# Mixture-of-experts layer on one Trainium2 core: weight ring laid into the mixer's tiles, 17 steps of 128, 96+32 and 64+64 slots

## The chip, the cores and the metric

The kernel runs on 1 core of one Trainium2 chip. The metric is the device time of one execution in microseconds (us). Below, "step" is one pass through the expert loop, "tile of weights" is 1 MB (half of one expert's gate, up or down matrix), and "slot" is one row of an expert's batch of tokens.

## What is computed

Two layers over 512 latent tokens and 256 context tokens of width 1024 (layer 1's second part works on the 512 latent ones). Each layer has a mixer (attention, gating and neighbourhood branches, output projection, gated residual) and then a mixture of experts. The change touches the second part:

```
expert = two best of 8 experts in the best of 4 groups   # per token, 32 experts
hdn    = silu(xb @ w_gate[e]) * (xb @ w_up[e])           # 1024 -> 512
y      = hdn @ w_down[e]                                 # 512 -> 1024
out    = h + gate * sum over the token's two experts of (weight * y)
```

Everything is fp32. One expert has 3 matrices of 2 MB, so 6 tiles of 1 MB; 32 experts are 192 tiles, 201 MB, per layer, and every expert is read in every layer.

## The kernel before

**Router.** The mixer's last stage is an output projection in two column halves (lines 1405 to 1438); after each token tile of the second half the router's logits are added up in PSUM (line 1401). `Router.choose` (line 1521) then runs a chain of small VectorE operations with a few TensorE products between: the two experts of each token, each token's position within its expert (`pos_ps`, `pk`), the experts' counts and their ranks by count. The two experts with the numbers 0 and 1 are fixed (`NST = 2`): they get ranks 0 and 1 whatever their counts, so that their weights can be asked for before the routing is known. All others are ranked by count, and `eid` (line 1574) is the list of expert numbers by rank, from which the SyncE queue reads an expert's number with a register load (line 1722) before it issues that expert's weights. `fill` (lines 1513 to 1519) turns positions and ranks into the list of tokens of every step by a series of small TensorE products, and `index` (line 1607) writes it as integers `gi` (rows to gather) and `si` (rows to scatter to).

**Steps.** In layer 0 the first 8 ranks are solo steps of 128 slots (`SOLO`) and the other 24 make 12 pairs of 64 slots each: 20 steps. In layer 1 it is 6 solo steps and 13 pairs: 19 steps. The order starts with the two fixed experts, then mixes pairs and solos, and ends with a solo. Each step gathers its 128 rows (line 1787, GpSimd's indirect DMA), transposes them (line 1798, eight TensorE transposes), multiplies by gate and up (`gateup`, four half products through `product`, line 1808), and in the next step's time transposes the hidden rows (line 1827), multiplies by down (`down`, two halves) and scatters the rows (line 1844). In a pair the two experts' matmuls take 64 columns of TensorE each, the second at column 64 (`tile_position`), alternately for each slice k of the contraction. So the program on TensorE runs: products of step i, transposes for step i+1, down of step i-1.

**Weights.** `Stream` (line 1706) holds the tiles in order of use. A ring of 15 tiles (`RP, RE = 7, 8`) lies in pools of its own, which replace the mixer's. `ahead` (line 1742) is called behind every half product and asks for as many tiles as were used, all on SyncE's queue at line 1731. The tiles of the ring that the mixer's space gives up come free one by one during the output projection.

**Overflow.** Tokens beyond an expert's slots are worked off behind the last step in a loop (`For_i`), whose number of passes `further` (line 1617) computes.

Of the kernel before, what the change touches and what calls it, by code (L numbers as in the profile page):

```python
# [23 lines left out]
KC = 8  # L24
# [7 lines left out]
SOLO = (8, 6)  # L32
NST = 2
NOV = (23, 15)
# [78 lines left out]
def backbone(ctx: ExitStack, tc: tile.TileContext, a, out, dbg=None):  # L113
# [119 lines left out]
    def mixer(l, comb):  # L233
# [52 lines left out]
        def wsplit(i, most=2, way=0):  # L286

            while most and i not in gone:
                if i not in pre:
                    pump()  # L290
                pool = pool2["p"] if seq[i] in (("out", 2), ("out", 3)) else wp
                first = i not in ready
                if first:
                    ready[i] = (pool.tile([128, KC, 256], F32R, tag="wh", name="wh", bufs=2),
                                pool.tile([128, KC, 256], F32R, tag="wl", name="wl", bufs=2))
# [175 lines left out]
        vv = wp.tile([128, 4, 512], F32, name="vv", bufs=1) if last else vtile([128, 6, 512], "vv")  # L471
# [867 lines left out]
        wo = ts.enter_context(tc.tile_pool(name=f"wo{l}", bufs=1, side="left", reuse_waits="tile"))  # L1339
        pool2["p"] = wo  # L1340
# [65 lines left out]
        for n in range(2):  # L1406
# [34 lines left out]
        st.close()  # L1441
        route.stack = rqs
        return hs, route
# [17 lines left out]
    class Router:  # L1461


        def __init__(self, l, NT, rq):
# [3 lines left out]
            self.pos_ps, self.ips, self.rank_ps, self.erow_ps, self.cc = (  # L1468
                pi[:, :NT + 1], pi[:, NT + 1], pi[:, NT + 2], pi[:1, NT + 3], pi[:NE, NT + 4, 0:1])
# [7 lines left out]
            self.H = SOLO[l]  # L1477
            self.P = (NE - self.H) // 2
            self.ns = self.H + self.P
            self.gi = const.tile([C, SOLO[0] + (NE - SOLO[1]) // 2], I32, name="gi")[:, :self.ns]  # L1480
            self.si = const.tile([C, SOLO[0] + (NE - SOLO[1]) // 2], I32, name="si")[:, :self.ns]

# [30 lines left out]
        def fill(self, po, oh, out, n, pair=None):  # L1513

            up = [(out[:, :n], k, nt, slice(0, 128), slice(0, n)) for k in range(2) for nt in range(self.NT)]
            low = [(out[64:128, pair[0]], k, nt, slice(0, 64), pair[1]) for _, k, nt, _, _ in up] if pair else []
            parts = up[:1] + low + up[1:]
            for i, (o, k, nt, sl, cl) in enumerate(parts):
                PE.matmul(o, po[:, k, nt, sl], oh[:, k, nt, cl], start=(i == 0), stop=(i == len(parts) - 1))

        def choose(self):
# [39 lines left out]
            for nt in range(NT):  # L1561
                PE.matmul(self.cc, OHs[:, nt, :], onesb[:, 0:1], start=(nt == 0), stop=(nt == NT - 1))

# [11 lines left out]
            tmp = t_([2, NT, NE], "tmp")  # L1575
            V.tensor_mul(tmp, self.OH, self.pos_ps[:, None, :NT, :].to_broadcast([128, 2, NT, NE]))
            V.reduce_sum(self.pk, tmp, axis=AX.X)
            po = t_([2, NT, C], "po", F16)
            V.tensor_tensor(po, self.along(C), self.over(self.pk, C), op=ALU.is_equal)
# [4 lines left out]
            V.tensor_scalar(v, r, float(self.H), -64.0, op0=ALU.is_lt, op1=ALU.mult)  # L1584
            V.tensor_add(self.d, self.pk, v)
            V.tensor_scalar(v, self.d, 64.0, 99.0, op0=ALU.is_ge, op1=ALU.mult)
            V.tensor_add(r, r, v)
            oh = self.column(rp, r, NE, "oh")
            self.fill(po, oh, self.ips, self.ns, (slice(self.H, self.ns), slice(self.ns, NE)))
            self.index(rp, self.ips, self.ns, self.gi, self.si)  # L1590
# [16 lines left out]
        def index(self, rp, ps, n, gi, si):  # L1607

            ps = ps[:, :n]
# [7 lines left out]
        def further(self, rp):  # L1617
# [4 lines left out]
            most = -(-(NT * 128 - 64) // C)  # L1622
# [5 lines left out]
            V.tensor_scalar(past, self.rank, float(self.H), -64.0, op0=ALU.is_lt, op1=ALU.mult)  # L1628
            V.scalar_tensor_tensor(past, cnt, -64.0, past, op0=ALU.add, op1=ALU.add)
# [31 lines left out]
            V.tensor_scalar_add(d, d, -64.0)  # L1661
# [18 lines left out]
            self.index(rp, ips, nov, self.gv, self.sv)  # L1680


    def moe(l, hs, route):
# [4 lines left out]
        RP, RE = 7, 8  # L1688
        NRAW = RP + RE
        ms, es_ = ExitStack(), ExitStack()  # L1690
        p = ms.enter_context(tc.tile_pool(name=f"m{l}", bufs=1, side=SIDE[l][0], reuse_waits="tile"))
        ep = es_.enter_context(tc.tile_pool(name=f"e{l}", bufs=1, side=SIDE[l][1], reuse_waits="tile"))
        pp = es_.enter_context(tc.tile_pool(name=f"eps{l}", bufs=1, space=PSUM, reuse_waits="tile"))
        wview = [a[n][l].rearrange("e (p k) f -> e p k f", p=128) for n in ("w_gate", "w_up", "w_down")]
        KK = (8, 8, 4)
        H, P, ns = route.H, route.P, route.ns

        def raw_tile(tag):
            return p.tile([128, 2048], F32, tag=tag, name=tag, bufs=RP - 4 if tag == "ew" else 2)

        def ring(i):
            if i < RP:
                return raw_tile("ew" if i < RP - 4 else "en" if i < RP - 2 else "ex")
            return ep.tile([128, 2048], F32, tag="er", name="er", bufs=RE)

        class Stream:


            def __init__(self, units, regs=None):
                self.units, self.regs = units, regs  # L1710
                self.room = NRAW if regs is None else RE
                self.raw = {}
                self.nl = self.nu = 0

            def expert(self, x):

                if self.regs is not None:
                    return ds(self.regs[x], 1)
                if x < NST:
                    return slice(x, x + 1)  # L1720
                if x not in places:
                    places[x] = SP.value_load(route.eid[0:1, x:x + 1], min_val=0, max_val=NE - 1)
                return ds(places[x], 1)

            def loads(self, upto):
                while self.nl < min(upto, len(self.units)):
                    x, mat, half = self.units[self.nl]
                    kk = KK[mat] // 2
                    t = ring(self.nl % NRAW if self.regs is None else RP)
                    src = wview[mat][self.expert(x), :, half * kk:(half + 1) * kk, :]  # L1730
                    SP.dma_start(t.rearrange("p (k f) -> p k f", k=kk), src.rearrange("o p k f -> (o p) k f"))
                    self.raw[self.nl] = t.rearrange("p (k f) -> p k f", k=kk)
# [367 lines left out]
```

## Time and profile before

| what | value |
|---|---|
| median of 3 runs | 2704.84 us (2703.21 to 2708.1) |
| the profiled execution | 2701.97 us |
| its span on the core | 2700.2 us |
| TensorE busy | 2410.3 us (89%) |
| VectorE, ScalarE, GpSimd busy | 1145.2, 691.0, 442.7 us |
| mean granted TensorE clock | 0.963 |
| moved by DMA | 625.81 MB, mean 232 GB/s |
| read from HBM | 602.55 MB |

The span is the time from the first to the last event on the core; the execution's time has 1.8 us around it. TensorE (PE) has matmuls in the table of groups, and its weight loads run beside them. The share of busy time is a mean over the mixers and the expert layers, whose limits differ. The numbers by stretch stand below.

### The profile page before, as it was taken

To read this page: it belongs to the slowest core of one execution; us is meant where nothing else is said; L and a number is where in the kernel's file an instruction comes from. 1 tells how busy PE (TensorE), PEld (TensorE's weight loads), DVE (VectorE), ACT (ScalarE), POOL (GpSimd) and SP (SyncE) were. 2 spreads that over 40 slices of the span, in tenths; PEclk is the share of its full clock that TensorE was granted. 3 is DMA by queue.
4 is the path that set the end of the run, shared out by engine and by line. 5 is a ranking of instruction groups with operands and counts; after the bars stand their busy time and mean duration, and the time that the engine had idled before them with its cause. 6 is when DMAs were issued, how large, how long until landed. Compare 5 with 4: busy or idle time off the path is not lost. (4 is left out here: it accounts for less than half of the span.)

```text
span 2700.2 us, 33207 instructions
## 1 busy us (share of the span) xinstructions
PE 2410.3 (89%) x12789; PEld 1641.1 (61%) x12789; DVE 1145.2 (42%) x2076; ACT 691.0 (26%) x1350; POOL 442.7 (16%) x387
## 2 busy tenths in 40 slices
PE   5999899899999699999986899999999699998983
PEld 4888788788887443333334788887877543333331
DVE  3455768677745411111104647676554411110003
ACT  4234655522222100000002325555223100000001
POOL 0221210212211100100000313112332100000002
PEclk9999999999999799999997899999999799999997
DMA  5411211365424799999996411123554699999993
GB/s 240 125 56 37 70 59 44 126 222 173 150 100 182 255 352 420 420 421 418 411 410 247 156 63 52 36 89 129 214 193 166 257 342 419 419 416 412 411 415 147
DMA packets 118144, 625.81 MB, mean 232 GB/s; under 512 B 18880, under 2 KB 24768, under 8 KB 58976
## 3 DMA queue, kind: packets, MB, share of 16 engines
q1 hardware_dynamic: 93232, 576.61, 54.7%
q0 software_dynamic: 14528, 32.60, 3.5%
q10 hardware_dynamic: 10224, 14.46, 1.5%
q8 instruction: 102, 1.67, 0.3%
q14 instruction: 58, 0.48, 0.1%
HBM read 602.55 MB, written 40.96 MB: 238 GB/s over the span
## 5 line engine op out<-in xcount | busy, mean ns | idle before, releaser
L217 PE MATMUL pg<-xh,wh 128*128 128x512 f32 (+1 forms) x576 | 205.2, 356 | 0.0
L218 PE MATMUL pg<-xl,wh 128*128 128x512 f32 (+1 forms) x576 | 205.0, 356 | 0.0
L219 PE MATMUL pg<-xh,wl 128*128 128x512 f32 (+1 forms) x576 | 204.1, 354 | 0.0
L694 PE MATMUL pj<-xh,wh 128*128 128x512 f32 (+1 forms) x544 | 196.2, 361 | 7.5 <-DVE rt L814 2.8
L696 PE MATMUL pj<-xh,wl 128*128 128x512 f32 (+1 forms) x544 | 189.9, 349 | 1.4 <-DVE wl L638 1.4
L1844 POOL DMA_INDIRECT yb<-mx,si x39 | 41.9, 1075 | 901.1 <-DVE mx L1843 652.7
L695 PE MATMUL pj<-xl,wh 128*128 128x512 f32 (+1 forms) x544 | 189.1, 348 | 0.0
L1808 PE MATMUL pu<-er,mt 128*64 128x512 f32 (+1 forms) x560 | 159.5, 595 | 19.5 <-DMA er<-in_w_up 19.3
L1808 PE MATMUL pd<-er,mt 128*64 128x512 f32 (+1 forms) x568 | 171.3, 596 | 6.1 <-DMA er<-in_w_down 3.2
L350 DVE SCALAR_TENSOR_TENSOR jk<-wr,crow 128x1024 bf16<-128x1024 f32 x128 | 155.8, 1218 | 47.0 <-DMA wr<-in_w_adaT 44.7
L1821 DVE TENSOR_TENSOR mx<-mx,pu 128x512 f32<-128x512 f32 x39 | 26.8, 688 | 343.0 <-PE pu L1808 336.4
L1808 PE MATMUL pg<-er,mt 128*64 128x512 f32 (+1 forms) x488 | 157.9, 610 | 9.6 <-DMA er<-in_w_gate 9.6
L200 POOL TENSOR_TENSOR wl<-wr,wh 128x1024 fp32r<-128x1024 f32 x48 | 119.6, 2492 | 280.6 <-ACT wh L199 280.6
L1843 DVE COPY mx<-pd 128x512 f32<-128x512 f32 x39 | 27.0, 692 | 306.8 <-ACT mx L1842 298.9
L1820 ACT ACTIVATE mx<-pg 128x512 f32<-128x512 f32 x39 | 23.3, 597 | 479.5 <-PE pg L1808 479.5
L1307 ACT ACTIVATE sg<-pg 128x512 f32<-128x512 f32 x72 | 37.9, 527 | 369.0 <-PE pg L219 361.4
L923 PE MATMUL S<-K,Q 128*128 128x256 f32 (+3 forms) x544 | 117.9, 342 | 14.5 <-ACT E L961 6.1
L1830 DVE COPY mt<-trh 128x512 f32<-128x512 f32 x39 | 27.0, 691 | 240.8 <-PE trh L1827 240.8
L1808 PEld LDWEIGHTS pu<-er,mt 128*64 128x64 f32 (+1 forms) x560 | 50.5, 142 | 112.7 <-issue 74.7
L217 PEld LDWEIGHTS pg<-xh,wh 128*128 128x128 f32 x576 | 108.1, 188 | 17.4 <-issue 0.3
L218 PEld LDWEIGHTS pg<-xl,wh 128*128 128x128 f32 x576 | 108.7, 189 | 15.9
L219 PEld LDWEIGHTS pg<-xh,wl 128*128 128x128 f32 x576 | 108.1, 188 | 16.7
(373 smaller groups left out, 5347.4 us busy)
## 6 DMA issues: line engine op xcount, KB each, us to landing
er<-in_w_down SPq DMA_DIRECT2D x71, 1024.0 KB, 21.5
er<-in_w_up SPq DMA_DIRECT2D x70, 1024.0 KB, 20.4
er<-in_w_gate SPq DMA_DIRECT2D x61, 1024.0 KB, 20.9
wr<-in_w_in SPq DMA_DIRECT2D x54, 1024.0 KB, 4.8
wr<-in_w_adaT SPq DMA_DIRECT2D x80, 512.0 KB, 3.7
ew<-in_w_gate SPq DMA_DIRECT2D x28, 1024.0 KB, 21.1
ew<-in_w_up SPq DMA_DIRECT2D x26, 1024.0 KB, 21.9
ew<-in_w_down SPq DMA_DIRECT2D x24, 1024.0 KB, 21.6
```

The lines of the kernel that those rows point to most:

```text
L200: (eng or V).tensor_sub(lo, x, hi.bitcast(F32))
L217: PE.matmul(ps, lh, rh, start=(i == 0), stop=False)
L218: PE.matmul(ps, lh, rl, start=False, stop=False)
L219: PE.matmul(ps, ll, rh, start=False, stop=(i == n - 1))
L350: V.scalar_tensor_tensor(jk, ad["t"][:, i % 2 * D:(i % 2 + 1) * D], 1.0, ad["c"][:, s], op0=ALU.mult, op1=ALU.mult, accum_out=modT[al][:, ...
L694: PE.matmul(ps, lh, rh, start=(k == 0), stop=False)
L695: PE.matmul(ps, lh, rl, start=False, stop=False)
L696: PE.matmul(ps, ll, rh, start=False, stop=(k == KC - 1))
L923: PE.matmul(ps, q[:, m, part, c], K[:, m, ks], start=(part == 0), stop=(part == 1))
L1307: S.activation(sg[:, o:o + n], ps[:, :n], AF.Sigmoid)
L1808: PE.matmul(ps[r], lt[:, k0 + k, r], w[:, k, c], start=(k0 + k == 0), stop=(k0 + k == kk - 1), **pos)
L1844: G.indirect_dma_start(out=yb[l], out_offset=bass.IndirectOffsetOnAxis(ap=idx, axis=0), in_=y, in_offset=None, bounds_check=2 * TT - 1, oo ...
```

## The change

- **Steps.** 17 steps in both layers (`NS`). Ranks 0 and 3 (`ALONE`) are solo steps of 128 slots. Of the others the biggest, ranks 1, 2 and 4 onwards, six in layer 0 and eight in layer 1 (`WIDE`), get 96 slots and share their step with one of the six or eight smallest experts, which gets 32 slots. The rest are pairs of 64 slots: nine in layer 0 and seven in layer 1. Experts 0, 1, 2 are now fixed (`NST = 3`). The order is solo 0, the wide steps of ranks 1 and 2, then pairs with wide steps between and the second solo in the middle; the last step is a wide one.
- **Matmuls of a wide step.** For each k, `product` issues three: 64 columns at column 0 and 32 at column 64 for the big expert, 32 at column 96 for the small one.
- **The ring.** 16 tiles that lie in tiles of the mixer's own pools, plus 5 (layer 0) or 4 (layer 1) of a small pool. The first 16 units are all of fixed experts: gate and up of 0 and 1, down of 0, gate and up of 2, down of 1. `Stream` is made in the mixer's tail, which asks for 1 or 2 tiles behind its row loads, one more at token tiles 1 and 3 of the first half of the output projection and 4 at the last token tile of each half; the expert layer's start asks for the rest up to 16. From there a tile is asked for when the unit 16 places before it has been used.
- **The router's chain in three parts.** `choose` becomes a generator. Part one makes positions and the list of expert 0 alone, whose rows are gathered at once. Part two does ranks, `eid` and each token's column. Part three, behind step 0's first half product, runs `fill` for the other 16 steps (48 small products where there were 24 in layer 0, 32 for 16 in layer 1), then the lists and the gather of step 1.
- `room` gives 128, 96, 64 or 32 slots by rank, for the columns and for the overflow.

```diff
-SOLO = (8, 6)
-NST = 2
+WIDE = (6, 8)
+NST = 3
+ALONE = 3
+NS = NE // 2 + 1
...
+        ring = [(wx, "x", 1)] + ([(wp, "vv", 1)] if last else []) + [(wp, "wr1", 1), (wp, "wr0", 1)]
+        ring += [(wp, t, 2) for t in ("wh", "wl")] * 2 + [(wa, "o0", 1)] + [(wo, f"o{i}", 1) for i in (1, 2, 3)]
+        weights = Stream(l, route, plan_steps(l), ring)
+        weights.loads(2 if last else 1)
...
                 if n == 0 and nt in (1, 3):
                     wsplit(at["n"] + nt // 2)
+                    weights.loads(weights.nl + 1)
...
+                if nt == NT - 1:
+                    weights.loads(weights.nl + 4)
...
-        def fill(self, po, oh, out, n, pair=None):
+        def fill(self, po, oh, out, n, low=()):
-            up = [(out[:, :n], k, nt, slice(0, 128), slice(0, n)) for k in range(2) for nt in range(self.NT)]
-            low = [(out[64:128, pair[0]], k, nt, slice(0, 64), pair[1]) for _, k, nt, _, _ in up] if pair else []
+            kn = [(k, nt) for k in range(2) for nt in range(self.NT)]
+            up = [(out[:, :n], k, nt, slice(0, 128), slice(0, n)) for k, nt in kn]
+            lo = [(out[o:128, c], k, nt, slice(0, 128 - o), x) for o, c, x in low for k, nt in kn]
...
+        def room(self, v, r):
...
+            V.tensor_scalar(v, r, float(2 + self.W), None, op0=ALU.is_lt)
+            for x, op in ((NE - self.W, ALU.is_lt), (0, ALU.is_equal), (ALONE, ALU.is_equal)):
+                V.scalar_tensor_tensor(v, r, float(x), v, op0=op, op1=ALU.add)
...
+            oh = t_([2, NT, 1], "oh0", F16)
+            V.tensor_mul(oh, self.OH[:, :, :, 0:1], tokn[l].rearrange("p k (t o) -> p k t o", o=1))
+            self.fill(po, oh, self.ips0, 1)
+            self.index(rp, self.ips0, self.gi[:, 0:1], self.si[:, 0:1])
+            yield
...
+    def plan_steps(l):
...
+        W = WIDE[l]
+        solo = [((x, 0, 128),) for x in (0, ALONE)]
+        small = list(range(NE - W, NE))
+        wide = [((x, 0, 96), (small.pop(0), 96, 32)) for x in range(1, 2 + W) if x != ALONE]
+        pair = [((x, 0, 64), (x + NS - 2 - W, 64, 64)) for x in range(2 + W, NS)]
+        r = solo[:1] + wide[:2]
+        rest = [wide[2:], pair]
+        for i in range(len(pair)):
+            r.append(pair[i])
+            n = len(wide) - 2
+            r += wide[2 + i * n // len(pair):2 + (i + 1) * n // len(pair)]
+            if i == len(pair) // 2:
+                r.append(solo[1])
...
+        return r
...
+            fixed = [] if regs is not None else [u for u in use if u[0] < NST][:16]
+            self.units = fixed + [u for u in use if u not in fixed]
...
+        def ahead(self):
...
+            self.used.update(self.now)
+            self.now = []
+            n = len(self.ring)
+            while self.nl < len(self.units) and (self.nl < n or self.units[self.nl - n] in self.used):
+                self.loads(self.nl + 1)
...
-        st_ = Stream(order([members(j) for j in plan]))
-        st_.loads(6 * NST - 2)
-        route.choose()
-        st_.loads(NRAW)
+        st_.loads(16)
+        choice = route.choose()
+        next(choice)
...
             for k in range(n):
-                for i, w in enumerate(ws):
-                    r = slice(None) if len(ws) == 1 else HALVES[i]
-                    pos = {} if len(ws) == 1 else {"tile_position": (0, 64 * i)}
-                    PE.matmul(ps[r], lt[:, k0 + k, r], w[:, k, c], start=(k0 + k == 0), stop=(k0 + k == kk - 1), **pos)
+                for (_, o, r), w in zip(m, ws):
+                    for o, r in ((o, r),) if r != 96 else ((o, 64), (o + 64, 32)):
+                        pos = {} if r == 128 else {"tile_position": (0, o)}
+                        PE.matmul(ps[o:o + r], lt[:, k0 + k, o:o + r], w[:, k, c], start=(k0 + k == 0),
+                                  stop=(k0 + k == kk - 1), **pos)
...
         gather(xg[0], gi[:, 0:1])
+        next(choice)
         x = xpose(xg[0])
-        gather(xg[1], gi[:, plan[1]:plan[1] + 1])
...
-            def mid():
-                if i:
+            def mid(part):
+                if i == part == 0:
+                    assert next(choice, 0) == 0
+                    gather(xg[1], gi[:, plan[1]:plan[1] + 1])
+                if i and part == 1:
                     box["hh"] = hpose(hd)
```

On TensorE, at the first step of layer 0 with two experts, the rows before are these (`tr` are the transposes of gathered rows, `trh` of hidden rows, `pg` and `pu` the gate and up products, `pd` the down product; `ew`, `en`, `ex`, `er` are weight tiles):

```order
L1798 MATMUL tr<-ident,mx 128x128 x8
L1808 MATMUL pd<-er,mt 128x512 x8
L1808 MATMUL pg<-er,mt 64x512 x8
L1808 MATMUL pu<-er,mt 64x512 x8
L1827 MATMUL trh<-ident,mx 128x128 x4
L1808 MATMUL pg<-er,mt 64x512
L1808 MATMUL pg<-ew,mt 64x512
```

and with the change, whose first such step is the second of the layer:

```order
L1848 MATMUL pu<-ew,mt 128x512 x4
L1838 MATMUL tr<-ident,mx 128x128 x8
L1848 MATMUL pg<-ew,mt 64x512
L1848 MATMUL pg<-ew,mt 32x512 x2
L1848 MATMUL pg<-ew,mt 64x512
L1848 MATMUL pg<-ew,mt 32x512 x2
L1848 MATMUL pg<-ew,mt 64x512
L1848 MATMUL pg<-ew,mt 32x512 x2
```

A half product of a pair is eight matmuls of 64 columns; that of a wide step is four of 64 columns and eight of 32, in turns.

On SyncE's queue, where layer 0's first weights are asked for, the rows before are

```order
L1731 DMA er<-in_w_up 128x2048
L1731 DMA er<-in_w_down 128x2048 x2
L1722 TENSOR_LOAD eid
L1722 ISA x2
L1731 ISA
L1731 DMA er<-in_w_gate 128x2048
```

and with the change

```order
L1771 DMA ew<-in_w_up 128x2048
L1771 DMA ew<-in_w_down 128x2048 x2
L1771 DMA ew<-in_w_gate 128x2048
L1771 DMA ew<-in_w_up 128x2048
L1771 DMA ew<-in_w_gate 128x2048
L1771 DMA ew<-in_w_up 128x2048
L1771 DMA ew<-in_w_down 128x2048 x2
L1758 TENSOR_LOAD eid
L1758 ISA x2
L1771 ISA
L1771 DMA ew<-in_w_gate 128x2048
```

Ten tiles stand ahead of the first register load of `eid` before, sixteen with the change.

On VectorE, in layer 0's routing, from the ranks on (`route` is the router's scratch, `OH` the choice of each token), the rows before are

```order
L1571 TENSOR_SCALAR route<-io_79,route 32x32
L1574 CAST eid<-pps 1x32
L1576 TENSOR_TENSOR route<-OH,pps 128x384
L1577 TENSOR_REDUCE pk<-route 128x12
L1579 TENSOR_TENSOR route<-io_79,pk 128x1536
L1581 TENSOR_TENSOR route<-OH,pps 128x384
...
L1614 TENSOR_TENSOR gi<-route 128x20
```

and with the change

```order
L1588 TENSOR_TENSOR route<-OH,pps 128x384
L1589 TENSOR_REDUCE pk<-route 128x12
L1591 TENSOR_TENSOR route<-io_79,pk 128x1536
L1594 TENSOR_TENSOR route<-OH,tokn_81 128x12
L1644 TENSOR_SCALAR route<-pps 128x1
L1645 SCALAR_TENSOR_TENSOR route<-pps,route 128x1
L1646 TENSOR_SCALAR route<-pps 128x1
L1647 TENSOR_TENSOR gi<-route 128x1
L1648 CAST si<-route 128x1
L1600 SCALAR_TENSOR_TENSOR route<-pps,kcol 32x1
```

The positions (128x384, the reduction, 128x1536) moved ahead of the ranks (32x32 rows), and step 0's list `gi` comes before the ranks are begun.

## Rows read from the trace of the kernel before

**Rows 1.** Stretches: length; busy PE, PEld, DVE, ACT, POOL; PE clock, DMA share, GB/s.

```profile
840.00:902.00 62.00, 59.46 (x320) 50.27 (x318) 35.40 (x61) 10.08 (x24) 4.69 (x9) 1.00 0.45 156
902.00:935.00 33.00, 9.46 (x91) 8.30 (x91) 15.94 (x57) 2.19 (x4) 3.68 (x4) 0.52 0.83 321
935.00:980.00 45.00, 44.40 (x131) 20.11 (x132) 5.46 (x15) 4.82 (x7) 4.00 (x4) 0.97 0.80 262
980.00:1430.00 450.00, 419.69 (x1610) 165.75 (x1608) 56.74 (x109) 30.64 (x52) 34.17 (x32) 1.00 1.01 415
```

**Rows 2.** SyncE's queue, timeline (start us, us, operation): weight tiles asked for.

```profile
919.82 0.33 SPq L1731 DMA_DIRECT2D er<-in_w_gate  x1
973.95 3.91 SPq L1731 DMA_DIRECT2D er<-in_w_gate  x2
1405.66 10.30 SPq L1731 DMA_DIRECT2D er<-in_w_down  x5
2192.87 3.91 SPq L1731 DMA_DIRECT2D er<-in_w_gate  x2
2618.17 10.26 SPq L1731 DMA_DIRECT2D er<-in_w_down  x5
```

**Rows 3.** The page's list of DMA issues: KB each, median us to landing.

```profile
er<-in_w_down SPq DMA_DIRECT2D x71, 1024.0 KB, 21.5
```

**Rows 4.** TensorE, timeline: solo and pair steps of layer 1.

```profile
2154.39 4.44 PE L1808 MATMUL pg<-ew,mt 128*128 128x512 f32 x8
2158.67 3.60 PE L1808 MATMUL pu<-ew,mt 128*128 128x512 f32 x8
2162.10 3.60 PE L1808 MATMUL pg<-ew,mt 128*128 128x512 f32 x8
2170.63 3.67 PE L1808 MATMUL pg<-en,mt 128*128 128x512 f32 x8 [0.61 <-issue]
2192.77 3.65 PE L1808 MATMUL pg<-er,mt 128*64 128x512 f32 x16
2215.44 3.65 PE L1808 MATMUL pg<-ex,mt 128*64 128x512 f32 x16
```

**Rows 5.** Layer 0's routing and first step: VectorE, TensorE and GpSimd, timelines.

```profile
914.27 0.15 DVE L1565 SCALAR_TENSOR_TENSOR route<-pps,kcol 32x1 f32<-32x1 f32 x1 [1.23 <-PE pps L1562]
915.78 0.53 DVE L1576 TENSOR_TENSOR route<-OH,pps 128x384 f32<-128x384 bf16 x1
918.61 0.55 DVE L1581 TENSOR_TENSOR route<-OH,pps 128x384 f32<-128x384 bf16 x1
921.81 1.31 PE L1519 MATMUL pps<-route 128*128 128x20 f16 x24 [6.18 <-DVE route L1510]
924.83 1.10 POOL L1788 DMA_INDIRECT mx<-xs,gi  x1 [21.27 <-DVE route L1601]
933.23 1.97 PE L1798 MATMUL tr<-ident,mx 128*128 128x128 f32 x8 [10.11 <-DMA mx<-xs,gi]
935.14 4.78 PE L1808 MATMUL pg<-ew,mt 128*128 128x512 f32 x8
```

**Rows 6.** TensorE, timeline: the last down product of each layer.

```profile
1437.77 7.10 PE L1808 MATMUL pd<-er,mt 128*128 128x512 f32 x16 [1.45 <-issue]
2650.34 7.11 PE L1808 MATMUL pd<-er,mt 128*128 128x512 f32 x16 [1.45 <-issue]
```

**Rows 7.** TensorE, timeline: columns (128*64, 128*32) side by side, and a change of width.

```profile
25.60 2.12 PE L430 MATMUL adaps<-adw,cpad 128*32 128x128 f32 x64
1103.15 0.84 PE L1798 MATMUL tr<-ident,mx 128*128 128x128 f32 x6
1103.91 0.64 PE L1808 MATMUL pd<-ex,mt 128*64 128x512 f32 x1
1104.39 0.59 PE L1808 MATMUL pd<-ex,mt 128*64 128x512 f32 x1
```

**Rows 8.** The trace's DMA view, list of issues: the gathers.

```profile
mx<-xs,gi POOLq DMA_INDIRECT x39, 10.7
```

More of the change, by code (lines that the diff above doesn't have):

```diff
@@ L1338, in mixer, with second_tile @@
         ts = ExitStack()
-        wo = ts.enter_context(tc.tile_pool(name=f"wo{l}", bufs=1, side="left", reuse_waits="tile"))
-        pool2["p"] = wo
+        es_ = ExitStack()
+        wa = st.enter_context(tc.tile_pool(name=f"wa{l}", bufs=1, side="left", reuse_waits="tile"))
+        wo = es_.enter_context(tc.tile_pool(name=f"wo{l}", bufs=1, side="left", reuse_waits="tile"))
+        wx = es_.enter_context(tc.tile_pool(name=f"wx{l}", bufs=1, side="left", reuse_waits="tile"))
+        second = iter([(wa, "o0"), (wo, "o1"), (wo, "o2"), (wo, "o3")])
+        def second_tile(name):
+            p, tag = next(second)
+            return p.tile([128, KC, 256], F32R, tag=tag, name=name, bufs=1)
+        pool2["t"] = second_tile
         rp = ts.enter_context(tc.tile_pool(name=f"r{l}", bufs=1, side="left", reuse_waits="tile"))
@@ L1679, in further @@
             self.sv = const.tile([C, NOV[0]], I32, name="sv")[:, :nov]
-            self.index(rp, ips, nov, self.gv, self.sv)
-    def moe(l, hs, route):
+            self.index(rp, ips, self.gv, self.sv)
+    def plan_steps(l):
[12 more added lines that the diff above has]
+                r.append(solo[1])
+        assert sorted(x[0][0] for x in r) == list(range(NS)) and sorted(y[0] for x in r for y in x) == list(range(NE))
+        return r
@@ L1695, in moe @@
[L1695 to L1732, printed above, removed]
-                    self.nl += 1
-            def get(self, *want):
-                i = self.nu
-                assert self.units[i] == want, (self.units[i], want)
-                self.nu += 1
-                self.loads(i + 1)
-                return self.raw.pop(i)
-            def ahead(self):
-                self.loads(self.nu + self.room)
@@ L1745, in members @@
-        def members(j):
-            return (j,) if j < H else (j, j + P)
-        def order(steps):
-            def downs(m):
-                return [(x, 2, half) for half in range(2) for x in m]
-            r, prev = [], ()
-            for m in steps:
-                r += [(x, mat, half) for half in range(2) for mat in range(2) for x in m]
-                r += downs(prev)
-                prev = m
-            return r + downs(prev)
-        plan = list(range(NST))
-        solo, pair = list(range(NST, H)), list(range(H, ns))
@@ L1763, in moe @@
-        for i in range(len(pair)):
-            plan.append(pair[i])
-            if (i + 1) * len(solo) // len(pair) > i * len(solo) // len(pair):
-                plan.append(solo[(i + 1) * len(solo) // len(pair) - 1])
-        assert sorted(plan) == list(range(ns))
-        places = {}
+        ep = es_.enter_context(tc.tile_pool(name=f"e{l}", bufs=1, side="left", reuse_waits="tile"))
+        pp = es_.enter_context(tc.tile_pool(name=f"eps{l}", bufs=1, space=PSUM, reuse_waits="tile"))
+        st_.ring += [(ep, "er", (5, 4)[l])] * (5, 4)[l]
@@ L1770, in moe, with raw_tile @@
+        assert len(st_.ring) == 16
+        rows_ = {"en": [("wh", 2)], "ex": [("wl", 2)], "ew": [("vv" if last else "o0", 1), ("wr0", 1), ("wr1", 1)]}
+        held = {t: p for p, t, _ in st_.ring}
+        turn = {"n": 0}
+        def raw_tile(kind):
+            x = rows_[kind]
+            tag, bufs = x[turn["n"] % len(x)]
+            turn["n"] += kind == "ew"
+            return held[tag].tile([128, KC, 256], F32, tag=tag, name=kind, bufs=bufs).rearrange("p a b -> p (a b)")
         b0, b1 = [bt(i, [128, 3072], F32, "mx") for i in SH]
@@ L1814, in gateup @@
                 for mat, ps in ((0, pg), (1, pu)):
-                    product(ps, x, [st_.get(y, mat, half) for y in m], 4 * half, 4, KC)
+                    product(ps, x, m, [st_.get(y[0], mat, half) for y in m], 4 * half, 4, KC)
                     st_.ahead()
-                if half == 0 and mid is not None:
-                    mid()
+                    if mid is not None:
+                        mid(2 * half + mat)
             sl, hd = sl_[i % 2], hd_[i % 2]
@@ L1835, in down @@
             for half in range(2):
[L1836 removed]
+                ws = [st_.get(y[0], 2, half) for y in m]
                 for o in range(2):
                     c = slice(o * 512, o * 512 + 512)
[L1839 removed]
+                    product(pd[:, c], ht, m, ws, 2 * half, 2, 4, c)
                 st_.ahead()
```

141 lines of the change are left out of this document (88 added, 53 removed).

## The prediction, made before the changed kernel ran

> **What bounds the kernel now.** I read first the busy time by stretch [rows 1]. The change touches only the expert layers, so the question is what limits those. From 980 to 1430 us of layer 0 the DMA engines are full (share 1.01, 415 GB/s), while TensorE is busy 419.69 of 450 us: the weights set the pace. Only the first two steps, 935 to 980, are the other way round: TensorE is busy 44.40 of 45 us and the DMA moves 262 GB/s. Before them, from 902 to 935, the router's chain runs, and TensorE has 9.46 us of work in 33.
>
> The second view is SyncE's queue [rows 2], which tells when the DMA becomes the limit. The ring is full at 919.82, before the first product; from then on a tile is asked for when one was used. The 26th is asked for at 973.95 + 3.91 - 0.33 = 977.53, which is 42.4 us after the first product at 935.14 [rows 5]; in layer 1 at 2196.45, 42.1 us after 2154.39 [rows 2, 4]. From there the queue never runs dry: the last ask is at 1405.66 + 10.30 - 0.33 = 1415.63, and 21.5 us later [rows 3] it has landed, at 1437.1. The tiles 26 to 192, 167 of them, took 459.6 us, **2.752 us each**. Layer 1 gives 2628.10 + 21.5 = 2649.6, and 2.713 us each. The five asks at the end are (10.30 - 0.33)/4 = 2.49 us apart; what is above that, 0.26 us x 167 = 44 us, is the share of the gathered and scattered rows, 2.4 us for each of some 18 steps.
>
> Third, TensorE's steps [rows 4]. A solo step 0 takes 2170.63 - 2154.39 = 16.2 us, the next 22.1, a pair step 22.7. A half product of 8 matmuls of 128 columns takes 3.43 us (2158.67 to 2162.10, when its successor starts; 8 x 0.43), and 16 matmuls of 64 columns are 3.65 us of busy time against 3.60 to 3.67 for 8 of 128: two of 64 columns run side by side. A pair needs 12 tiles, 12 x 2.49 + 2.4 = 32.3 us of DMA, against 22.7 us of TensorE.
>
> So fewer steps save TensorE time that nobody waits for. What can change is the start (when the flood of weights begins), the end, and TensorE becoming the limit.
>
> **The change, part by part.**
>
> *Start of the flood.* All 192 tiles are still read. The 32nd tile is now asked for when the 16th unit, expert 1's second down half, has been used: behind step 0, the second step with its down, and the third step's products and down, 16.2 + 22.1 + 15.6 + 7.1 = 61.0 us after the first product (15.6 is a step of 22.7 without its 7.1 of down, rows 4 and 6). [rows 4, 6] In step 0 the 48 small products of the lists now run between two half products: 24 took 1.31 us [rows 5], so 2.6. From there 161 tiles x 2.752 = 443.1. First product to last landing: 61.0 + 2.6 + 443.1 = 506.7 in place of 42.4 + 459.6 = 502.0, **+4.7 us** in layer 0. Layer 1: 61.0 + 2.0 + 161 x 2.713 = 499.8 against 42.1 + 453.1 = 495.2, **+4.6**. The deeper ring doesn't shorten anything that ends last: the first tiles are there either way.
>
> *First product.* Expert 0's list needs the positions only. They took 915.78 to 918.61, 2.83 us, behind 914.27, when the ranks began [rows 5]. Put in the ranks' place: 914.27 + 2.83, one small multiply 0.2, half of 1.31 for 12 products, and the 1.7 from there to the gather (923.12 to 924.83), near 919.8: **5.0 us earlier**, and all that follows with it. That holds if the gather lands as long after its issue as now, 933.23 - 924.83 = 8.4; the median over all steps is 10.7 [rows 8], and the stretch already has a DMA share of 0.83 [rows 1], so the gain has the bounds 0 (every microsecond is lost again in a fuller queue) and 5. I take 5.0 in layer 0, and 4 in layer 1, where two thirds of the tokens go through the chain. More weight tiles are asked for before the router ends; in the out-projection the DMA share is 0.45 [rows 1], which is their cover. Without it they would land late by what is over the ring's end, at most the 2.5 us of one tile.
>
> *Rows beside the weights.* The rows of one or two steps more now move before the flood. Bounds 0 and 2 steps more (4.8); I take **-3** a layer.
>
> *End.* The last down of layer 0 runs 1437.77 + 7.10 = 1444.87 [rows 6], 7.8 us after the last landing; in layer 1 2657.45, 7.9. That step is a solo, whose down follows the whole down of the pair before it. With a step of two experts last, its four down tiles come at 2.49 us apart, after the step before has done its own, and only the last half is left after the last landing: 3.5 us. **-4.3** a layer.
>
> *Queues.* SyncE has sixteen tiles instead of ten ahead of its first wait for the list of experts. What queues behind that wait are only dynamic experts' tiles, the first needed 16.2 us after the first product, as before. On GpSimd the second gather is asked for in step 0 instead of ahead of it: some 3.4 + 2.6 + 1.7 = 7.7 us after the first product, and with 8.4 us to land it is there at 16.1, when the second step's transposes want it. At 10.7 [rows 8] it costs 2.3.
>
> *Matmuls of a wide step.* Per k there is a 64-column tile, two of 32 and, for fp32, two passes of each. If the three go side by side, a wide step costs what a pair does, 22.7 us, less than its 32.3 us of DMA. The trace shows side by side for 64 columns alone [rows 4] and for 32 alone: 64 records in 2.12 us [rows 7], 0.033 each; their moving tile has 128 columns, and a quarter of the 0.43 us that 512 take would be 0.107, so three to four run at a time. It has no place where both widths alternate. Lower bound: 0.86 us per k, as a pair. Upper bound: the widths follow each other and each change costs what a change from 128 to 64 columns shows. There [rows 7] six transposes begin at 1103.15, 0.11 apart, and the next product not at 1103.81 but at 1103.91, and its first pass takes 0.48 instead of 0.43: 0.15 us a change. With two changes per k that is 4 x 0.43 + 2 x 0.15 = 2.02 us. I take the lower end, as the nearest rows are products of columns that don't overlap and that run side by side.
>
> The Trainium skill, page "TensorEngine Tiling (Array Packing)", section "Key Properties", says that a change of tiling mode drains TensorE, and lists 128x64 and 128x32 as two modes; the same section says that different tiles work in parallel. By its first sentence the upper end would hold, by its second the lower one. The trace agrees with the first for a change to 64 columns from 128; no run here shows 64 against 32.
>
> **Sum.** Layer 0: +4.7 - 5.0 - 3 - 4.3 = -7.6. Layer 1: +4.6 - 4 - 3 - 4.3 = -6.7. Against the profiled execution's 2701.97 us: 2687.7; that execution stands 2.9 below the median of 2704.84, so I forecast **2690.5 us**. Its own range, with the gather's gain at 0 or full and the rows at 0 or 4.8, and 3 us either way for the start of the flood: 2678 to 2706.
>
> **Rivals.**
>
> *1. The widths don't run together, and TensorE becomes the limit (slower).* Place: the products of the 14 wide steps. 24 k-slices at 2.02 us, plus 2.1 of transposes and gaps, make 50.6 us a wide step against 32.3 of DMA. It decides from the point where a wide step passes the DMA's 32.3, so from 1.26 us per k. Layer 0, from the first product at 930.1: 16.2 + 2.6 + 6 x 50.6 + 10 x 22.7 = 549.4, end at 1479.5 instead of 1444.87, +34.6. Layer 1, from 2150.4: 16.2 + 2 + 8 x 50.6 + 8 x 22.7 = 604.6, 2755.0 instead of 2657.45, +97.5. Together +132, 2837 us. Without any cost for the change itself (1.72 per k, 43.4 us a step) the same sums give 2737, with a change at every pass (57.8 us a step) 2938. For it: the 0.15 us change in rows 7, and that the program alternates widths at every k. Against it: the columns are apart.
>
> *2. The start eats the gains (no change).* The first gather lands no earlier for the weights in its way, the second lands late by 2.3 us, the flood begins 4.7 later. The end's -8.6 and -3 for the rows remain, against +9.3 and twice +2.3: 2701.97 + 2.3 + 2.9 = 2707, between 2699.5 and 2710 by what of each comes true.
>
> *3. An expert has more tokens than its slots (slower).* Each overflow pass is a step of its own at the end, with nothing beside it: 10.7 of gather, six tiles at 2.49, 16.2 + 7.1 of TensorE [rows 4, 6, 8], near 50 us. Counting the router's choices by the reference's own formulas, the most is 96 in layer 0 and 90 in layer 1, both at rank 3, which has 128 slots; the 96-slot experts have 91 at most, the six or eight smallest 31. So nothing should overflow: 2740 with one pass, unlikely.
>
> **How the numbers follow.** Chances: forecast 0.50, rival 1 0.36, rival 2 0.11, rival 3 0.03. A measurement of this kernel can tell some 0.2% from no change, 5.4 us here. Of the forecast 0.45 is faster by more and 0.05 within; rival 2 gives 0.02, 0.08 and 0.01; rivals 1 and 3 are slower. Faster 0.47, same 0.13, slower 0.40. The range begins at 2676 and goes up to 2860: below lies 0.04, above it what rival 1 has over its middle value, 0.13. The cases of both signs are both in it; the likeliest one's own range is the one given with the sum.
>
> **What the profile after would show.** If the forecast holds: in a wide step the three matmuls of a k start within hundredths of a microsecond, a wide half product takes 3.4 to 3.7 us, DMA share stays at 1.0 to the end of each layer, and TensorE's busy share falls. The first gather is issued near 919.8, and the last down ends 3.5 us after the last weight's landing. If rival 1 holds: a wide half product takes 7 to 8 us, the DMA share falls well under 1 in the second half of each layer, and SyncE's asks wait for TensorE. If the loop at the end runs, rival 3. A first product no earlier than 935 would break the second term, a 32nd tile asked for much before 61 us after the first product the first.

## The result: 5.4% slower, by the mechanism of the first rival

The changed kernel takes 2851.55 us (median of 4 runs, 2850.95 to 2853.44) against 2705.1; the ratio is 1.0541 with a 95% interval of 1.0523 to 1.056. The forecast was 2690.5, faster; the first rival said 2837. The profiled execution has a span of 2849.2 us against 2700.2, and its busy time by stretch reads (columns as in [rows 1]):

```profile
902.00:928.00 26.00, 8.83 (x80) 7.87 (x80) 15.77 (x54) 0.58 (x1) 2.99 (x4) 0.52 0.86 354
980.00:1430.00 450.00, 440.92 (x1670) 126.70 (x1670) 49.93 (x108) 24.82 (x43) 29.23 (x27) 1.00 0.94 386
2600.00:2780.00 180.00, 180.00 (x636) 43.53 (x634) 12.06 (x18) 8.25 (x14) 8.04 (x8) 1.00 0.83 333
```

In the same 450 us of layer 0 TensorE is now busy 440.92 us instead of 419.69 and the DMA share has fallen from 1.01 to 0.94; in layer 1 TensorE is busy all of 180 us and the DMA share is 0.83. The bound has moved from the weights to TensorE. TensorE's timeline at layer 0's start and at the end of both layers, against [rows 4 to 6]:

```profile
926.10 1.97 PE L1838 MATMUL tr<-ident,mx 128*128 128x128 f32 x8 [5.88 <-DMA mx<-xs,gi]
928.00 4.83 PE L1848 MATMUL pg<-ew,mt 128*128 128x512 f32 x8
932.66 1.69 PE L1537 MATMUL pps<-route 128*128 128x17 f16 x48
934.21 3.68 PE L1848 MATMUL pu<-ew,mt 128*128 128x512 f32 x8
...
946.26 7.98 PE L1848 MATMUL pg<-ew,mt 128*64 128x512 f32 x24 [0.61 <-issue]
954.17 8.01 PE L1848 MATMUL pu<-ew,mt 128*64 128x512 f32 x24
962.11 0.75 PE L1868 MATMUL trh<-ident,mx 128*128 128x128 f32 x4
...
979.66 7.03 PE L1848 MATMUL pd<-ew,mt 128*128 128x512 f32 x16
986.63 8.01 PE L1848 MATMUL pg<-ew,mt 128*64 128x512 f32 x24
...
1036.03 3.65 PE L1848 MATMUL pg<-ew,mt 128*64 128x512 f32 x16
...
1468.99 7.09 PE L1848 MATMUL pd<-ew,mt 128*64 128x512 f32 x32
1478.20 15.92 PE L1848 MATMUL pd<-ew,mt 128*64 128x512 f32 x48 [1.44 <-issue]
...
2201.11 4.86 PE L1848 MATMUL pg<-ew,mt 128*128 128x512 f32 x8
...
2791.67 15.92 PE L1848 MATMUL pd<-ew,mt 128*64 128x512 f32 x48 [1.44 <-issue]
```

A wide half product takes 7.94 us from start to start (954.17 to 962.11), where a pair's takes 3.5 (each fp32 matmul stands as two records, its two passes: the 24 are 12 matmuls), and the wide down 15.92 where the pair's takes 7.09. SyncE's queue shows the last fixed tiles of the ring and, later, asks at TensorE's pace:

```profile
912.53 1.12 SPq L1771 DMA_DIRECT2D ew<-in_w_down  x2
...
994.66 8.27 SPq L1771 DMA_DIRECT2D ew<-in_w_gate  x2
1011.22 8.27 SPq L1771 DMA_DIRECT2D ew<-in_w_up  x2
```

From 994.66 on two tiles are asked for 7.94 us apart (8.27 less the 0.33 that one takes), which is a wide half product. The first gather:

```profile
919.73 1.10 POOL L1828 DMA_INDIRECT mx<-xs,gi  x1 [15.84 <-DVE route L1603]
```

The waits of TensorE in layer 1 (2240 to 2780 us; operation, waited for, us in total, times, longest) say the same:

```profile
PE pu L1848 <- DMA ew<-in_w_up: 0.7, 1, 0.7
PE pd L1848 <- DMA ew<-in_w_down: 0.5, 1, 0.5
PE pg L1848 <- DMA ew<-in_w_gate: 0.4, 1, 0.4
```

In 540 us TensorE waits 1.6 us for weights. Where the 149 us come from, by the starts of the first and last operation of each stretch in the traces (us; the last two columns are two kernels of the experiments below):

| stretch | before | change | three tiles of 32 | free places |
|---|---|---|---|---|
| to the last router logit, layer 0 | 906.7 | 907.0 | 910.7 | 906.7 |
| to the first product | 28.4 | 21.0 | 20.6 | 21.5 |
| to the last down product | 509.1 | 565.5 | 502.6 | 490.8 |
| to layer 1's first transpose | 20.3 | 20.9 | 21.6 | 21.6 |
| to the last router logit, layer 1 | 664.5 | 669.8 | 672.3 | 666.9 |
| to the first product | 25.3 | 16.9 | 17.2 | 16.4 |
| to the last down product | 502.5 | 605.9 | 497.3 | 486.8 |
| to the end | 43.3 | 42.2 | 42.5 | 42.4 |

The expert loops cost 56.4 and 103.4 us more; the shorter way to the first product gives 7.4 and 8.4 back, and layer 1's mixer, which the change doesn't mean to touch, is 5.3 longer.

### The profile page after: what moved, and what is told of

It reads as the page before. It is cut to its first block, busy times and chain, and to the rows that moved or that the text cites. A ratio compares the mean times of both kernels' runs of the same rounds, so it can differ in the third digit from the quotient of the medians.

```text
span 2849.2 us, 34410 instructions
## 1 busy us (share of the span) xinstructions
PE 2634.5 (92%) x13461; PEld 1584.8 (56%) x13461; DVE 1136.0 (40%) x2082; ACT 682.1 (24%) x1335; POOL 433.5 (15%) x377
## 5 line engine op out<-in xcount | busy, mean ns | idle before, releaser
L1848 PE MATMUL pg<-ew,mt 128*64 128x512 f32 (+2 forms) x1248 | 376.3, 606 | 4.3 <-DMA ew<-in_w_gate 3.1
L1848 PE MATMUL pu<-ew,mt 128*64 128x512 f32 (+2 forms) x1248 | 373.5, 602 | 3.7 <-DMA ew<-in_w_up 3.7
L1848 PE MATMUL pd<-ew,mt 128*64 128x512 f32 (+2 forms) x1248 | 369.2, 603 | 6.8 <-DMA ew<-in_w_down 3.9
L1848 PEld LDWEIGHTS pu<-ew,mt 128*64 128x64 f32 (+2 forms) x1248 | 87.7, 129 | 278.5 <-issue 267.6
L1848 PEld LDWEIGHTS pd<-ew,mt 128*64 128x64 f32 (+2 forms) x1248 | 87.0, 129 | 263.7 <-issue 250.6
L1848 PEld LDWEIGHTS pg<-ew,mt 128*64 128x64 f32 (+2 forms) x1248 | 85.7, 130 | 261.1 <-issue 250.1
L1861 ACT ACTIVATE mx<-pg 128x512 f32<-128x512 f32 x34 | 20.3, 597 | 540.7 <-PE pg L1848 540.7
L926 PE MATMUL S<-K,Q 128*128 128x256 f32 (+3 forms) x544 | 117.6, 341 | 14.3 <-ACT E L964 5.9
## 6 DMA issues: line engine op xcount, KB each, us to landing
ew<-in_w_up SPq DMA_DIRECT2D x128, 1024.0 KB, 15.1
```

Of the source, the lines that this page charges most:

```text
L926: PE.matmul(ps, q[:, m, part, c], K[:, m, ks], start=(part == 0), stop=(part == 1))
L1848: PE.matmul(ps[o:o + r], lt[:, k0 + k, o:o + r], w[:, k, c], start=(k0 + k == 0), stop=(k0 + k == kk - 1), **pos)
```

## Experiments

All are timed against the kernel before, run on the same chip beside them. The first four ask what makes the wide steps dear.

**Three tiles of 32.** The 96 columns as three tiles of 32, so that a k has four tiles of one width:

```diff
-for o, r in ((o, r),) if r != 96 else ((o, 64), (o + 64, 32)):
+for o, r in ((o, r),) if r != 96 else ((o, 32), (o + 32, 32), (o + 64, 32)):
```

> The changed kernel, with the 96 columns of a wide step as three tiles of 32, so that all four tiles of a k have one width. Theory A (tiles of 64 and of 32 columns don't run together): the wide half product falls from 7.94 to 3.4 to 3.7 us, DMA is the limit again, and the time is the forecast's, 2680 to 2700 us. Theory B (the cost goes with the number of matmuls, 32 instead of 24 in a half product): the half product rises to 10.6 us and the time to about 3070. Theory C (the loss lies elsewhere: ring in the mixer's tiles, split router, other order): the half product falls and the time stays near 2850.

Measured: 2681.93 us (4 runs), ratio 0.9911 (0.9894 to 0.9928). TensorE's timeline, layer 0's first gather and the ask for the 32nd tile (the second of the two), and TensorE's waits for weights from 990 to 1430 us:

```profile
931.26 5.54 PE L1848 MATMUL pg<-ew,mt 128*128 128x512 f32 x8
...
950.23 3.64 PE L1848 MATMUL pg<-ew,mt 128*32 128x512 f32 x32 [0.61 <-issue]
953.66 3.64 PE L1848 MATMUL pu<-ew,mt 128*32 128x512 f32 x32
...
1426.72 7.74 PE L1848 MATMUL pd<-ew,mt 128*32 128x512 f32 x64 [1.41 <-issue]
```

```profile
923.37 1.10 POOL L1828 DMA_INDIRECT mx<-xs,gi  x1 [15.76 <-DVE route L1603]
```

```profile
992.34 3.77 SPq L1771 DMA_DIRECT2D ew<-in_w_gate  x2
```

```profile
PE pu L1848 <- DMA ew<-in_w_up: 26.4, 19, 1.9
PE pg L1848 <- DMA ew<-in_w_gate: 26.0, 22, 2.2
PE pd L1848 <- DMA ew<-in_w_down: 10.8, 13, 1.6
```

32 matmuls take less than half of what 24 took, and TensorE waits for the weights again, 63 us in 440. So theory A holds; the count of matmuls (B) and the rest of the change (C) are not the loss.

**Widths grouped.** In each `product` of a wide step all 64-column tiles first, then all of 32:

```diff
...
+if m[0][2] == 96:
+    todo = ([(k, ws[0], 0, 64) for k in range(n)] +
+            [(k, w, o, 32) for k in range(n) for w, o in ((ws[0], 64), (ws[1], 96))])
...
```

> The changed kernel, with a half product's 64-column tiles all ahead of its 32-column tiles. Theory A: the two widths still follow each other, only fewer changes: a gate or up half product is 4 x 4 x 0.43 + 2 x 0.13 = 7.1 us instead of 7.94, and the time 2790 to 2815 us. Theory A2 (64 and 32 would run together, and only the change of width at every k costs): the half product falls to 3.7 to 4.5 and the time to about 2700. Theory B: 24 matmuls as before, 7.9 us, 2850.

Measured: 2808.36 us (one run).

```profile
948.31 7.18 PE L1850 MATMUL pg<-ew,mt 128*64 128x512 f32 x24 [0.61 <-issue]
955.42 7.21 PE L1850 MATMUL pu<-ew,mt 128*64 128x512 f32 x24
```

7.11 us from start to start: the 6.88 of 16 passes one behind the other, and 0.23 for two changes of width. So fewer changes save 0.83 us of a half product, and the other passes still stand one behind the other. That alone doesn't show that the two widths can't overlap: this order puts products on the same columns next to each other, and no run shows whether later ones on other columns could pass them. The rows of the mixed widths below show it, where neighbours lie on separate columns. Taken together, 3.44 of the 4.5 us that a wide half product costs more are missing overlap, and the changes at every k are the rest.

**96 + 32 multiplied as 64 + 64**, the control:

```diff
+o, r = {96: (0, 64), 32: (64, 64)}.get(r, (o, r))
...
```

> The changed kernel, with the wide steps' 96 + 32 columns multiplied as 64 + 64 (slots 64 to 95 get the other expert's weights, so this part of the result is left out); all else as in the change. Theories A and B: 16 matmuls of 64 columns in a half product, 3.5 us, time as in the run with three tiles of 32 under A, 2680 to 2700 us. Theory C: near 2850 in spite of it.

Measured: 2683.22 us (one run), the same as with three tiles of 32, so four tiles of 32 cost no more than two of 64.

**Mixed widths in the kernel before**, with nothing else of the change:

```diff
 for i, w in enumerate(ws):
-    r = slice(None) if len(ws) == 1 else HALVES[i]
+    for o, r in ((0, 128),) if len(ws) == 1 else ((0, 64),) if i == 0 else ((64, 32), (96, 32)):
...
```

> The kernel before, with the second expert of each pair as two tiles of 32 columns; nothing else changed. Theory A: a half product of a pair takes 7.9 us instead of 3.5, a pair step 50, TensorE is the limit: layer 0 is 16.2 + 7 x 22.1 + 12 x 50 = 771 us from first product to last instead of 510, layer 1 16.2 + 5 x 22.1 + 13 x 50 = 777 instead of 503, together about 3240 us. Theory C: no change, 2705.

Measured: 3242.14 us (one run). Here the timeline shows the two widths apart:

```profile
992.75 1.07 PE L1808 MATMUL pg<-er,mt 128*64 128x512 f32 x2
993.75 1.05 PE L1808 MATMUL pg<-ew,mt 128*32 128x512 f32 x4
994.74 1.07 PE L1808 MATMUL pg<-er,mt 128*64 128x512 f32 x2
995.74 1.05 PE L1808 MATMUL pg<-ew,mt 128*32 128x512 f32 x4
```

Two passes of 64 columns, then the four records of 32 (two tiles, side by side, two passes), 1.0 us each: 2 x 0.43 and 0.13 to 0.14 for the change. The 32s, on columns of their own, start only when both passes of the 64s are over. By itself this puts 536 us on a kernel that is otherwise the one before. The wide steps' widths are the cause of the loss: taken out of the change it is gone, put into the kernel before it appears, both at the computed size.

**Packed lists.** The next two ask for layer 1's mixer, 5 to 8 us longer in every run of the change. Its matmuls start 234 ns apart where they started 229, 232 and 226 (medians of 192 each in the traces of layer 1's gate projection, for the three products of a split pair); layer 0's are unchanged. The change's longer overflow lists move all later tiles by 96 bytes, but layer 1's split weights, which are laid out from the other end, stay.

```diff
+gs = const.tile([C, 2, NS], I32, name="gs")
+self.gi, self.si = gs[:, 0], gs[:, 1]
...
+ov = const.tile([128, 3, NOV[0]], I32, name="ovi")[:, :, :nov]
+self.ebi, self.gv, self.sv = ov[:, 0], ov[:, 1], ov[:, 2]
```

> The kernel with three tiles of 32, and six small lists of the router packed into two tiles, which takes 96 bytes off the tiles ahead of the mixer's big ones, so that these begin at the same address (46624 instead of 46720) as in the kernel before. Theory P (the layer-1 mixer takes 670 to 672 us in all runs of the change against 663 to 664.5 without it because its operands were shifted by 96 bytes while its weight tiles were not): first transpose to last logit of layer 1 falls from 672.3 to 663 to 665 us, and the median from 2682 to 2673 to 2677. Rival: the mixer is slower for another reason (tiles held by the ring, queue order): nothing changes.

**The kernel before, moved by 96 bytes:**

```diff
-self.ebi = const.tile([128, NOV[0]], I32, name="ebi")[:, :nov]
+self.ebi = const.tile([128, 25], I32, name="ebi")[:, :nov]
...
```

> The kernel before, with three lists of the overflow two words longer, so that all tiles behind them begin 96 bytes later, as in the change; nothing else changed. Theory P: the layer-1 mixer takes 670 to 672 us instead of 664, and the median rises from 2706 to 2712 to 2714. Rival: no change.

Layer 1's mixer, first transposes and last logits, in the kernel before, in the kernel before moved, and with the lists packed:

```profile
1464.57 3.78 PE L487 MATMUL nt<-ew,hr 128*128 128x128 f32 x16 [19.70 <-DVE ew L1948]
...
2125.99 3.54 PE L1404 MATMUL lps<-rw,xt 128*128 128x36 f32 x16
```

```profile
1465.93 3.78 PE L487 MATMUL nt<-ew,hr 128*128 128x128 f32 x16 [19.78 <-DVE ew L1948]
...
2132.92 3.63 PE L1404 MATMUL lps<-rw,xt 128*128 128x36 f32 x16
```

```profile
1448.71 3.58 PE L490 MATMUL nt<-ew,hr 128*128 128x128 f32 x16 [20.69 <-DVE ew L1993]
...
2109.84 3.63 PE L1421 MATMUL lps<-rw,xt 128*128 128x36 f32 x16
```

661.4 us, 667.0 and 661.1: moved, the mixer of before is 5.6 us longer, with 234 ns from start to start; packed, the change's is back at 229, 232 and 226 ns. On the whole time it shows less clearly: the moved kernel takes 2707.32 us, ratio 1.0012 (1.0002 to 1.0022), and the packed one 2677.14, ratio 0.9901 (0.9884 to 0.9917) against 0.9911 unpacked, intervals that overlap. Other things move this mixer too: in the last kernel below, packed as well and with 229, 232 and 226 ns again, the stretch of the table above takes 666.9 us where the packed one's takes 664.3. Which operand's address counts, and why, wasn't tried.

**The router's parts together.** The next three measure terms of the prediction on the kernel with three tiles of 32.

```diff
+next(choice)
+assert next(choice, 0) == 0
 gather(xg[0], gi[:, 0:1])
-next(choice)
+gather(xg[1], gi[:, plan[1]:plan[1] + 1])
...
```

> The kernel with three tiles of 32, with the router's three parts run together ahead of the first gather, and both first gathers behind them. Theory S (what the first product gains or loses in time moves the layer's end): the time from the last logit to the first product rises from 20.6 and 17.2 us to 27 to 29 and 24 to 26, less the 2.6 and 2 us of list products that no longer stand between two half products; median 2692 to 2697. Rival (the weights set the pace and hide it): 2682.

Measured: 2686.69 us, ratio 0.9935 (0.9918 to 0.9951), between the two, with an interval that overlaps that of the split router. It doesn't test what it meant to: GpSimd waits for expert 0's list alone, and the first gather still goes out 12.6 us after the last logit (920.74 against 908.1). Only the other lists' products moved, from step 0 to ahead of it, where they hold up the transposes by 1.6 us.

**Expert 0's list last.** So its four lines were moved behind the other lists, and the second gather goes out right behind the first:

```diff
...
 self.index(rp, self.ips[:, 1:NS], self.gi[:, 1:NS], self.si[:, 1:NS])
+oh = t_([2, NT, 1], "oh0", F16)
+V.tensor_mul(oh, self.OH[:, :, :, 0:1], tokn[l].rearrange("p k (t o) -> p k t o", o=1))
+self.fill(po, oh, self.ips0, 1)
+self.index(rp, self.ips0, self.gi[:, 0:1], self.si[:, 0:1])
...
```

> The kernel with three tiles of 32, with expert 0's list made behind the lists of all other steps, so that the first gather waits for the whole of the router's chain as in the kernel before (the earlier try left the first gather waiting for its own list alone). Theory S (a later first product moves the layer's end, since the ring is full and the DMA idle by then): last logit to first product rises from 20.6 and 17.2 us to 28 to 31 and 23 to 26, less 1.6 and 1.1 us of list products that leave step 0; median about 2694 to 2699. Rival (the weights hide it): 2682.

Measured: 2692.63 us, ratio 0.9957 (0.9941 to 0.9974), by medians 10.7 us above the split router and by the ratios 12.4, as the two ran on different chips. The first gather and product:

```profile
928.62 1.10 POOL L1826 DMA_INDIRECT mx<-xs,gi  x1 [24.25 <-DVE route L1632]
```

```profile
933.01 1.97 PE L1836 MATMUL tr<-ident,mx 128*128 128x128 f32 x8 [6.02 <-DMA mx<-xs,gi]
934.91 4.88 PE L1846 MATMUL pg<-ew,mt 128*128 128x512 f32 x8
```

First products come 27.2 and 22.9 us after the last logit instead of 20.6 and 17.2, 12.3 us together, and the end moves with them but for 2.2 us. Theory S holds.

**Solo step last.** The second solo step at the end instead of in the middle:

```diff
-            if i == len(pair) // 2:
-                r.append(solo[1])
+        r.append(solo[1])
```

> The kernel with three tiles of 32, with the second solo step as the last step instead of in the middle. Theory L (the last step's down is what is left after the last landing: 3.7 us with two experts, 7.8 with one): each layer ends 3.5 to 4.3 us later, median 2688 to 2691. Rival: the end is set by the landing alone, 2682.

Measured: 2691.74 us, ratio 0.9955 (0.9939 to 0.9972); first product to last down 507.0 and 502.2 us, 4.4 and 4.9 more than with a wide step last. Theory L holds, a little above its numbers.

**Free places.** In the change a tile waits for the place 16 before it in the order of loads. Since fixed experts' tiles lead that order, places freed by others in steps 1 and 2 stay empty. Here a tile takes the place freed first (on the packed kernel):

```diff
+def free(self):
+    late = self.regs is None and self.nl >= len(self.units) - 8
+    r = [(self.when[self.live[t][0]], i) for i, (_, t, _) in enumerate(self.ring)
+         if self.live[t][0] in self.when and not (late and t in ("wh", "wl"))]
+    return min(r)[1] if r else None
...
-pool, tag, bufs = self.ring[self.nl % n]
+i = self.nl if self.nl < n else self.free()
+pool, tag, bufs = self.ring[i]
...
```

> The packed kernel with three tiles of 32, in which a tile of weights goes to whichever place of the ring was freed first, not to the one 16 places before it in the order of loads; so that the tiles freed in steps 1 and 2 are asked for at once. Theory F (the flood's start, now 64 us after the first product, counts in full): the queue is never dry from the second step on, some 20 us after the first product; 172 tiles x 2.70 us from there give a last landing 487 us after the first product instead of 499.5, 12 us less in each layer, median 2650 to 2658. Rival (what is asked for earlier only waits longer in the queue): 2677.

Measured: 2654.41 us (4 runs), ratio 0.9818 (0.9802 to 0.9835), the fastest of the study and faster than both kernels. Stretches of this kernel, and of the packed one without it (columns as in [rows 1]):

```profile
925.00:945.00 20.00, 18.76 (x93) 9.99 (x94) 2.76 (x15) 4.07 (x6) 2.00 (x2) 0.88 0.50 169
945.00:990.00 45.00, 44.39 (x354) 16.34 (x356) 8.07 (x21) 3.53 (x6) 3.01 (x3) 1.00 0.99 405
```

```profile
925.00:945.00 20.00, 19.39 (x113) 9.70 (x116) 3.13 (x15) 4.66 (x7) 3.00 (x3) 0.97 0.68 232
945.00:990.00 45.00, 45.00 (x354) 15.99 (x348) 8.01 (x23) 3.54 (x6) 2.10 (x3) 1.00 0.87 292
```

In the 45 us that follow step 0 the DMA moves 405 GB/s instead of 292; from first product to last down the loops take 490.8 and 486.8 us in place of 502.4 and 498.4 in the packed kernel, 11.6 less each, where 12 were computed. What is left is the time of step 0, with a DMA share of 0.50.

## Why the prediction was wrong

**The step that failed** is the one on the matmuls of a wide step: "I take the lower end, as the nearest rows are products of columns that don't overlap and that run side by side". Those rows show products of one width. The ends of that estimate were right: 0.86 us per k was taken, 2.02 was the upper one, and 7.94/4 = 1.985 was measured. I weighed distinct columns above a row of the trace that showed a change of width costing something [rows 7]. The Trainium skill's rule in "TensorEngine Tiling (Array Packing)", section "Key Properties", that a change of tiling mode drains TensorE, decides for the upper end here, and this case's traces agree: 0.13 us a change, and no overlap across it. The Trainium skill's other rule there, that different tiles work in parallel, holds here within one width alone (four tiles of 32 in 3.43 us a half product).

**The rival that came true** was sized well, in part by luck. Layer 1's loop was to take 604.6 us and ends 2791.67 + 15.92 - 2201.11 = 606.5 after its first product. Two errors of that sum nearly cancel: it leaves out the down product of step 0 (979.66 to 986.63, 7.0 us in layer 0), and it takes 50.6 us for a wide step with its down that takes 49.4 (986.63 to 1036.03). Layer 0's was put at 549.4 and takes 566.1. With both errors put right it would be 18.3 (928.00 to 946.26) + 7.0 + 6 x 49.4 + 10 x 22.7 = 548.7, and most of what is above that is waiting for weights. There nine pairs stand between six wide steps, and the two limits alternate: a wide step lets the queue fill, the pairs behind it empty it again and then wait. TensorE's waits in the changed kernel, 980 to 1430 us, columns as above:

```profile
PE pd L1848 <- DMA ew<-in_w_down: 3.4, 4, 1.3
PE pu L1848 <- DMA ew<-in_w_up: 3.0, 2, 1.7
PE pg L1848 <- DMA ew<-in_w_gate: 2.7, 3, 1.3
```

These 9.1 us are the part that stands as idle time. A sum that takes TensorE's time alone leaves the waits out. The second rival's sum has a slip too: it takes the -3 of the rows once, where the forecast takes it in each layer, and would be 2704 instead of 2707.

**The other terms** can be read in the run with three tiles of 32, which is what the forecast assumed. Its median is 24.2 us below the kernel before beside it, its profiled span 15.5; the sum was -14.3. That these lie so close is luck: by the table, first products and loops gained 27.6 us, nearly twice the sum, and the mixers and the rest, which the sum leaves out, took some 12 back.

- First product, -5.0 and -4: measured -7.8 and -8.1. The gather's issue came earlier as computed, at 919.73 in the changed kernel (919.8 predicted). The rest is its landing: the product starts 7.9 us after the gather's issue (923.37 to 931.26) in place of 10.3 [rows 5]. The ring's last five tiles used to wait for the list of experts, the last of them until 919.82 [rows 2], 5.0 us ahead of the gather; with three fixed experts none of the ring waits for it, and in the changed kernel the last is asked for at 913.0 (the second of the two from 912.53), 6.7 us ahead. The run with expert 0's list last fits this: the same asks, a gather 15.1 us behind the last of them, and its product 6.3 us later (928.62 to 934.91). No run moved the asks alone, so that they are the cause is argued and not shown. The bound "0 to 5" left out that a gather can also get faster.
- Start of the flood, 63.6 us after the first product: measured 995.78 - 931.26 = 64.5. This was right, though the 48 small products in step 0 took 1.55 us (932.66 to 934.21 in the changed kernel) and not 2.6. That it was a flaw of the order and not of the ring's size, I didn't see; the free places took it away.
- Rows and end, -3 and -4.3 a layer: with the flood's start the loop was to be 2.6 us shorter, and is 6.5 and 5.2. In the traces the last tile lands 499.5 and 494.2 us after the first product, where it was 501.3 and 494.2 before and the sum had it 1.7 and 1.6 later: the 161 tiles from the 32nd on took 2.70 and 2.68 us each, rows included, where the sum's 2.752 and 2.713 with 3 us taken off come to 2.73 and 2.69. The last down product then starts 3.1 us after the landing in place of 7.8 and 8.3, so the end gave 4.8 and 5.2 instead of 4.3; the solo step put last bears that out with 4.4 and 4.9.
- Nothing in the prediction costed the mixer, which lost 5 to 8 us; the moved kernel shows 5.6 of them for the addresses. The diff showed the longer lists, but no row of the trace connects them with it.

## What to carry to other kernels

Before column tiles of different widths are mixed, look for a place in a trace where exactly those widths alternate. Where there is none, take the widths as one behind the other, or cut all to the narrowest, which cost nothing here. Where weights are the limit, fewer steps gain little by themselves. What counts is when the queue is first full for good, and what is left to do behind the last landing; a place in a ring should go to the next tile the moment it is free.

## What the runs showed of the hardware

- In these fp32 products of 512 columns, tiles 64 and 32 wide don't overlap, on separate columns either: 16 passes of 0.43 us follow each other, and a change between these widths adds 0.13 us. Four tiles of 32 side by side take the time of two of 64, 3.43 us a half product.
- Moving one side's operands of unchanged matmuls by 96 bytes made them start 234 instead of 226 to 232 ns apart, and a mixer of 661 us 5.6 us longer. The reason stays open.
- In layer 0 the first gather was followed by its product 10.3 us later where the last of the ring's tiles had been asked for 5.0 us ahead of it, 8.3 (changed kernel) where it was 6.7, and 6.3 (list last) where it was 15.1. The cause is not shown by a run of its own.
